# Rotary rows of the input projections in chunks of their own, and operands parked in DRAM as (halves, rows, heads)

## The chip, the cores and the metric

One core of one Trainium2 chip. The time is device microseconds (us) of one execution. TensorE (PE) multiplies matrices; PEld is its weight load; VectorE (DVE), ScalarE (ACT) and GpSimd (POOL) do the elementwise work; SyncE (SP) issues the transfers (DMAs). Below, an instruction is named by its engine and its line in the listing (DVE L782 is VectorE's work on line 782 of the kernel before; the same code stands some 30 lines lower in the kernel after).

## What is computed

A decoder trunk of two layers over 512 tokens of width 1024. Each layer is x += 0.5 SwiGLU(norm x), a mixing stage, and another half-step SwiGLU. The change is in the mixing stage:

```
h = rmsnorm(x, mix_norm[l]) @ w_in[l]                 # 2290 columns
h_a, h_b, h_c = split(h)                              # three groups of heads
o = concat([mla(h_a), nsa(h_b), diff(h_c)]);  x = x + o @ w_out[l]
# nsa:  q (6 heads x 64), kc, ks, kw (2 x 64 each): rotary on the first 16 of 64 dims
# diff: q, k (4 heads x 2 x 32): rotary on the first 8 of 32 dims; then scores,
#       p = p1 - lambda * p2, and p @ v
def apply_rope(x, cos, sin):                          # x1, x2: first and second half of the dims
    return concat([x1 * cos - x2 * sin, x1 * sin + x2 * cos])
```

## The kernel before

Everything is kept transposed: a tile has 128 features on its partitions and the 512 tokens along it. Products in float32 are made of halves: a number is split into a high half (an ACT cast, `split`, L146) and the rest (a subtraction, L148 or, with a scale, L150, on DVE or POOL), and three matrix products are added.

The mixing stage projects 16 chunks of 128 columns of `w_in` (`project`). A projection ends in PSUM and goes through a function `done`. Chunks 3 to 5 hold the queries of the nsa heads, 6 and 7 their keys ks and kw, 8 kc, 9 vc; chunks 12 and 13 hold the queries of the diff heads, 14 and 15 their keys. For chunks 3 to 8 and 12 to 15 `done` is a rotary step (`rope`): a shuffle of partitions from PSUM (DVE L525), PSUM times cos (DVE L526), the shuffled rows times sin (L527) and the sum (L528). The last two run on POOL for chunks 3 to 8 and on DVE for 12 to 15. cos and sin come from DRAM (`tabs`) and are first multiplied by the norm's factor on POOL (`tables`, L535, twice for each of two pairs of tables in a layer). Rows that have no rotary dims go through the same four instructions with cos = 1 and sin = 0. The result is halved and parked in DRAM (`park`, one transfer), and read back in the layout in which the heads need it (`c_load`, `b_queries`, `b_keys`, `compress`).

After the four diff chunks and the values `cv` the program runs through `PLAN`, a table of periods written by hand. A period names the head whose scores are made (front), the head whose probabilities are turned and weighed (back), the order of front steps (f), back steps (b) and other work (.), and what that work is: `p2` or `b8` are projections of chunks, `cl1` is the load of diff head 1, `aq0` a query of the mla heads. Matmuls keep this order; the order on the other engines is made by the compiler's scheduler. The first four periods, c0 to c3, are the diff heads. In each, two softmaxes are combined by DVE L782 (`c_front`), and PE then turns the result (L551) and weighs it (`c_back`).

In layer 1 an ACT table set with exp and ln is preloaded after the last SiLU of the FFN. SyncE issues all transfers in order, and all kinds share its queue: weights, parked tiles, `tabs`.

Of the kernel before, what the change touches and what calls it, by code (L numbers as in the profile page):

```python
# [47 lines left out]

C_ID, C_ONE, C_BLK, C_MSK, C_CM, C_C01, C_FRQ, C_SGN, C_END = 0, 128, 256, 384, 512, 640, 768, 771, 774
# [38 lines left out]
def tile_hybrid_trunk(ctx: ExitStack, tc: tile.TileContext, I, out, dbg=None):  # L88
# [429 lines left out]
    SWAP16 = [(i + 16) % 32 for i in range(32)]  # L518
    SWAP8 = [i + 8 if i < 8 else i - 8 if i < 16 else i for i in range(32)]
    SWAP4 = [i + 4 if i < 4 else i - 4 if i < 8 else i for i in range(32)]  # L520

    def rope(src, cos, sin, swap, r0=0, r1=P, eng=gp):
# [127 lines left out]
    def mix(l, xn, nxt):  # L650
# [45 lines left out]
        def scaled(pj, by):  # L696
            t = tmp()
            ve.tensor_tensor(t, pj, by, op=ALU.mult)
            return t

        def halves(t, scale=None, eng=ve):
            hl = btile()
            n = t.shape[0]
            split(t, hl[:n, 0], hl[:n, 1], scale, eng)
            return hl

        def park(t):
# [30 lines left out]
        def c_init():  # L738
            S["tab"] = tables(2, rs[0])
            dl = small([P, 4, 32], "dl", bufs=1)  # L740
# [13 lines left out]
        def c_done(c, eng=gp):  # L754
            def done(pj):
                if "tab" not in S:
                    c_init()
                S[c] = park(halves(rope(pj, *S["tab"], SWAP4, eng=eng), C_SCALE if c < 14 else None))
            return done

        def c_load(h):
            a, s = h // 2, h % 2
# [166 lines left out]
        def b_rope(c):  # L929
            def done(pj):  # L930
                if "tabb" not in S:
                    S["tabb"] = tables(1, rs[0])
# [3 lines left out]
        def b_token():  # L936
            def done(pj):
                S["b", 9] = park(halves(scaled(pj, rs[0]), eng=gp if "h9" in SPARE else ve))
            return project(9, done)

        def compress(n):
            d, phi, pe_t = (S["b", 8], I["phi_k1"], I["pe_k"]) if n == "k" else (S["b", 9], I["phi_v1"], I["pe_v"])
            pt = small([64, 32], "pe", bufs=1)
# [4 lines left out]
            k = xt.rearrange("p j (g n) -> p j g n", g=2)  # L948
            src = d.rearrange("(g d) j n -> d j g n", g=2)
            pb = ph.unsqueeze(2).broadcast_to([64, 2, 2, 32])  # L950
# [32 lines left out]
        def b_queries(i):  # L983
            q = pair("qk")
            src = S["b", 3 + i].rearrange("(s d) j n -> j d s n", s=2)
            for j in range(2):
                move(q[64 * j:64 * j + 64], src[j])
            S["q", 2 * i], S["q", 2 * i + 1] = q[:, 0], q[:, 1]
# [58 lines left out]
        def b_keys(c, g):  # L1047
            k = S["k", c, g] = btile()
            for d in range(2):
                S["last"] = move(k[64 * d:64 * d + 64], S["b", 6 + c][64 * g:64 * g + 64])  # L1050

# [105 lines left out]
def _consts():  # L1157
# [9 lines left out]
    for t in range(NT):  # L1167
# [4 lines left out]
        c[:, C_C01 + 32 * t:C_C01 + 32 * t + 32] = ok  # L1172
    for g, (inv, per) in enumerate(((INV_A, 32), (INV_B, 64), (INV_C, 32))):
        n = len(inv)
        for p in range(P):
            r = p % per
            if r < 2 * n:
                c[p, C_FRQ + g] = inv[r % n]
                c[p, C_SGN + g] = -1.0 if r < n else 1.0
    return c  # L1180


def _lay(inputs):
# [68 lines left out]
```

## Time and profile before

| | us |
|---|---|
| median of 3 runs | 2050.43 (2048.09 to 2051.41) |
| profiled execution, its own time | 2050.42 |
| its span, first to last instruction | 2048.6 |
| PE busy | 1977.7 |
| DVE busy | 1498.9 |
| ACT busy | 1082.3 |
| POOL busy | 309.6 |

The profiled execution is as good as the median, and 1.8 us of its time lie outside the span. The two mixing stages run from about 361 to 690 us and from about 1373 to 1705 us; the rest is FFN. PE, the engine with the most work, is idle in 70.9 us of the span.

### The profile page before, as it was taken

To read this page: it belongs to the slowest core of one execution; us is meant where nothing else is said; L and a number is where in the kernel's file an instruction comes from. 1 tells how busy PE (TensorE), PEld (TensorE's weight loads), DVE (VectorE), ACT (ScalarE), POOL (GpSimd) and SP (SyncE) were. 2 spreads that over 40 slices of the span, in tenths; PEclk is the share of its full clock that TensorE was granted. 3 is DMA by queue.
4 is the path that set the end of the run, shared out by engine and by line. 5 is a ranking of instruction groups with operands and counts; after the bars stand their busy time and mean duration, and the time that the engine had idled before them with its cause. 6 is when DMAs were issued, how large, how long until landed. Compare 5 with 4: busy or idle time off the path is not lost.

```text
span 2048.6 us, 31102 instructions
## 1 busy us (share of the span) xinstructions
PE 1977.7 (97%) x11864; PEld 1720.7 (84%) x11864; DVE 1498.9 (73%) x2339; ACT 1082.3 (53%) x2023; POOL 309.6 (15%) x217
## 2 busy tenths in 40 slices
PE   8999999978999999999999999999889999999997
PEld 6899988856777899998889999888667778999886
DVE  8888863688897888883378887337888888888623
ACT  4455632476677645562254556225656774555521
POOL 5000011245520100001100000112555110000011
PEclk9999999999999999999999999999989999999999
DMA  6333354623541523335442334446336234233431
GB/s 206 103 108 111 117 180 130 201 91 110 142 155 38 189 93 106 110 118 145 130 134 89 108 107 131 129 138 189 114 100 191 80 124 139 93 104 104 129 116 54
DMA packets 93316, 253.84 MB, mean 124 GB/s; under 512 B 13936, under 2 KB 17776, under 8 KB 93168
## 3 DMA queue, kind: packets, MB, share of 16 engines
q1 hardware_dynamic: 93168, 251.87, 39.6%
q8 instruction: 93, 1.52, 0.3%
q14 instruction: 55, 0.45, 0.1%
HBM read 219.94 MB, written 29.88 MB: 122 GB/s over the span
## 4 chain that ended last, share of the span: by engine, by line
PE 83%; DVE 10%; ACT 3%; POOL 2%; issue 1%; DMA 1%; SPq 0%; DVEq 0%; ACTq 0%; POOLq 0%
PE psm L540 20%; PE psm L175 13%; PE pss L540 11%; PE pst L175 9%; PE pst L540 8%; PE pss L175 8%; PE pso L540 6%; PE pso L175 5%; PE pst L551 1%; DVE pn L782 1%; DVE nmx L573 1%; DVE b L150 1%; DVE pt L148 1%; ACT pn L574 1%; POOL t L270 1%
## 5 line engine op out<-in xcount | busy, mean ns | idle before, releaser
L146 ACT CAST whl<-raw 128x1024 fp32r<-128x1024 f32 (+2 forms) x417 | 383.8, 922 | 512.1 <-issue 107.4
L148 DVE TENSOR_TENSOR whl<-raw,whl 128x512 fp32r<-128x512 f32 (+2 forms) x373 | 409.8, 1100 | 233.3 <-ACT whl L146 232.6
L540 PE MATMUL psm<-b,whl 128*128 128x256 f32 (+1 forms) x2140 | 450.6, 347 | 9.2 <-DVE t L905 8.9
L540 PEld LDWEIGHTS psm<-b,whl 128*128 128x128 f32 x2140 | 329.9, 192 | 51.9 <-DVE t L905 10.7
L270 POOL TENSOR_TENSOR t<-t,t 128x512 f32<-128x512 f32 x48 | 78.8, 1641 | 1104.9 <-ACT t L264 793.8
L175 PE MATMUL psm<-b,whl 128*128 128x512 f32 (+1 forms) x948 | 230.8, 383 | 1.5 <-DVE whl L148 1.0
L175 PEld LDWEIGHTS psm<-b,whl 128*128 128x128 f32 x948 | 174.6, 189 | 36.8 <-DVE whl L148 1.4
L175 PE MATMUL pst<-b,whl 128*128 128x512 f32 x624 | 157.8, 393 | 2.5 <-ACT whl L146 1.3
L574 ACT ACTIVATE pn<-pss,nmx 128x256 f32<-128x256 f32 x208 | 109.9, 529 | 65.7 <-DVE nmx L573 64.5
L175 PEld LDWEIGHTS pst<-b,whl 128*128 128x128 f32 x624 | 117.5, 189 | 29.3 <-ACT whl L146 1.8
L573 DVE TENSOR_REDUCE nmx<-pss 128x1 f32<-128x256 f32 x208 | 97.7, 484 | 40.8 <-PE pss L540 26.5
L175 PE MATMUL pss<-b,whl 128*128 128x512 f32 x504 | 126.4, 389 | 0.0
L540 PE MATMUL psm<-qk,whl 128*128 128x256 f32 x840 | 123.6, 283 | 0.0
L540 PE MATMUL pst<-b,whl 128*128 128x256 f32 (+1 forms) x816 | 121.1, 290 | 0.2 <-DVE b L148 0.2
L540 PE MATMUL pss<-b,whl 128*128 128x256 f32 (+1 forms) x816 | 120.8, 289 | 0.0
L540 PEld LDWEIGHTS psm<-qk,whl 128*128 128x128 f32 x840 | 111.1, 192 | 0.3
L175 PEld LDWEIGHTS pss<-b,whl 128*128 128x128 f32 x504 | 94.6, 188 | 19.6
L540 PEld LDWEIGHTS pst<-b,whl 128*128 128x128 f32 x816 | 108.5, 192 | 2.9 <-DVE b L148 0.5
L540 PEld LDWEIGHTS pss<-b,whl 128*128 128x128 f32 x816 | 108.9, 192 | 2.1
L148 POOL TENSOR_TENSOR whl<-raw,whl 128x1024 fp32r<-128x1024 f32 (+4 forms) x44 | 83.3, 1897 | 172.5 <-ACT whl L146 150.5
L148 DVE TENSOR_TENSOR whl<-pn,whl 128x1024 fp32r<-128x1024 f32 x63 | 77.2, 1225 | 26.3 <-ACT whl L146 26.3
L551 PE MATMUL pst<-cst,pn 128*128 128x128 f32 x440 | 78.0, 292 | 13.0 <-DVE pn L782 7.1
(316 smaller groups left out, 3538.9 us busy)
## 6 DMA issues: line engine op xcount, KB each, us to landing
raw<-in_ffn_gu_dram SPq DMA_DIRECT2D x174, 512.0 KB, 3.7
raw<-in_ffn_d_dram SPq DMA_DIRECT2D x64, 512.0 KB, 3.8
park<-b SPq DMA_DIRECT2D x30, 512.0 KB, 3.7
raw<-in_w_in_dram SPq DMA_DIRECT2D x28, 512.0 KB, 3.7
raw<-in_ffn_d_dram SPq DMA_DIRECT2D x32, 384.0 KB, 3.2
xin<-xs SPq DMA_DIRECT2D x48, 256.0 KB, 3.1
raw<-in_w_out_dram SPq DMA_DIRECT2D x32, 256.0 KB, 2.6
xs<-t SPq DMA_DIRECT2D x24, 256.0 KB, 2.4
```

Source lines behind the costliest of these rows:

```text
L146: high = sc.copy(hi, src) if scale is None else sc.mul(hi, src, scale)
L148: eng.tensor_tensor(lo, src, f32(hi), op=ALU.subtract)
L150: eng.scalar_tensor_tensor(lo, src, scale, f32(hi), op0=ALU.mult, op1=ALU.subtract)
L175: pe.matmul(ps, w(a), x(b), start=first and k == 0 and j == 0, stop=last and k == n - 1 and j == 2)
L270: gp.tensor_tensor(sq, sq, self.acc, op=ALU.add)
L540: return tc.keep_in_program_order(pe.matmul(*args, **kw))
L551: return tc.keep_in_program_order(pe.transpose(dst, src, idn))
L573: ve.reduce_max(nmx, part[i], axis=AX.X, negate=True)
L574: sc.activation(pn[i], part[i], AF.Exp, bias=nmx, accum_out=sm[:, i:i + 1])
L782: ve.scalar_tensor_tensor(p1[j], p1[j], s1[:, j:j + 1], p2[j], op0=ALU.mult, op1=ALU.add)
```

## The change

The columns of `w_in` are put in another order, so that the rotary rows lie together: the diff heads' in chunk 12, the nsa queries' and kc's in chunk 3, the keys' in chunk 6. Only these three chunks get a rotary step (`roped`: PSUM times the norm's factor first, then shuffle, cos, sin and sum out of SBUF, with the plain tables). The other chunks are only multiplied by the norm's factor (`scaled`, one DVE instruction). `tables` and its POOL products go. Scales that differ by row come from a column of constants. Tiles are parked by `put` into tensors shaped (halves, rows, tokens), in which a head's rows lie so that the reads are plain; a chunk is put in two to four pieces. Every diff head now has rows in all four chunks 12 to 15, so that `c_load(0)` stands behind the last of them. `PLAN` swaps b8 with b3 and b3 with b4, and c0 has another order. In `rotary` the last Sin is noted as the activation that the preload has to follow.

```diff
-    ("c0", "", "f.f..fb.f..f.b.bf..bb...", "p2 p0 cl1 cl2"),
-    ("c1", "c0", "f.f..b..ff.f..fbb..bb...", "lat p1 b8 cl3 an"),
+    ("c0", "", "...f.f..f.f..f..f..", "p2 p0 cl1 cl2"),
+    ("c1", "c0", "f.f..b..ff.f..fbb..bb...", "lat p1 b3 cl3 an"),
     ("c2", "c1", "ff....fbf..f.bb..f.bb...", "t9 ak0 av0"),
-    ("c3", "c2", "ff...f.bf.f..bbf..bb...", "b4 aq0 cn0 aq1 b5 b3"),
+    ("c3", "c2", "ff...f.bf.f..bbf..bb...", "b8 aq0 cn0 aq1 b5 b4"),
...
-            sc.activation(h, r, AF.Sin, scale=0.5)
+            last_silu[0] = sc.activation(h, r, AF.Sin, scale=0.5)
...
-    def tables(g, by):
-
-        t = btile(F32)
-        for j in range(2):
-            gp.tensor_tensor(t[:, j], loaded(tabs[g, j]), by, op=ALU.mult)
-        return t[:, 0], t[:, 1]
...
+        def roped(pj, g, swap, n=P, eng=gp):
+
+            t = scaled(pj, rs[0])
+            c, sw = tmp()[:n], tmp()[:n]
+            ve.stream_shuffle(sw, t[:n], swap)
+            ve.tensor_tensor(c, t[:n], loaded(tabs[g, 0])[:n], op=ALU.mult)
+            eng.tensor_tensor(sw, sw, loaded(tabs[g, 1])[:n], op=ALU.mult)
+            eng.tensor_tensor(t[:n], c, sw, op=ALU.add)
+            return t
...
+        def put(part, at, t, r, n):
+
+            return sy.dma_start(part[:, at:at + n].rearrange("j p n -> p j n"), f32(t[r:r + n]))
...
-                S[c] = park(halves(rope(pj, *S["tab"], SWAP4, eng=eng), C_SCALE if c < 14 else None))
+                t = halves(roped(pj, 2, SWAP8, eng=eng) if c == C_TOP else scaled(pj, rs[0]), scales(0))
+                for i in range(2):
+                    put(S["C"][i], 64 * (c - C_TOP), t, 64 * i, 64)
...
-                src = S[12 + 2 * c + a][64 * s:64 * s + 64].rearrange("(m r) j n -> j r m n", m=2)
+                src = S["C"][c].rearrange("j (d h m) n -> j d h (m n)", h=4, m=2)[:, :, h]
+                dst = qk[c].rearrange("p m n -> p (m n)")
                 for j in range(3):
-                    move(qk[c][32 * j:32 * j + 32], src[PASS[j][1 - c]])
+                    move(dst[32 * j:32 * j + 32], src[PASS[j][1 - c]])
...
-                S["b", c] = park(halves(rope(pj, *S["tabb"], SWAP8), B_SCALE if c < 6 else None, gp if "h%d" % c in SPARE else ve))
+                t = roped(pj, 1, SWAP16, P if c == 3 else 64) if c in (3, 6) else scaled(pj, rs[0])
+                scale = {3: scales(1), 8: scales(2), 4: B_SCALE, 5: B_SCALE}.get(c)
+                t = halves(t, scale, gp if "h%d" % c in SPARE else ve)
+                for r, n, p, at in B_PIECES[c]:
...
+                    put(S["part", p], at, t, r, n)
...
-        project2(12, 14)
-        c_load(0)
-        for c in (13, 15):
+        project2(C_TOP, C_TOP + 1)
+        for c in (C_TOP + 2, C_TOP + 3):
             for _ in project(c, c_done(c, ve), ve):
                 pass
+        c_load(0)
```

The order of instructions moves with it at three places. The first is SyncE's queue at the start of the first layer's diff heads: `park` tensors and `part` tensors hold the parked chunks, `qk` tiles are the operands of the heads (two for each head, three reads each). Before:

```order
L710 DMA park_3507<-b_3504 128x1024
L710 DMA park_3518<-b_3515 128x1024
L166 DMA qk_3520<-park_3507 32x2x512 x3
L160 DMA raw_4242<-in_w_a_dram 128x640
L166 DMA qk_3521<-park_3518 32x2x512 x3
L710 DMA park_3567<-b_3564 128x1024
L166 DMA qk_3875<-park_3507 32x2x512
L710 DMA park_3608<-b_3605 128x1024
L166 DMA qk_3875<-park_3507 32x2x512 x2
L166 DMA qk_3876<-park_3518 32x2x512 x3
L166 DMA qk_3883<-park_3567 32x2x512 x3
```
After:

```order
L739 DMA part_3479<-b_3505 64x2x512
L739 DMA part_3480<-b_3505 64x2x512
L739 DMA part_3479<-b_3512 64x2x512
L739 DMA part_3480<-b_3512 64x2x512
L739 DMA part_3479<-b_3549 64x2x512
L739 DMA part_3480<-b_3549 64x2x512
L174 DMA raw_4234<-in_w_a_dram 128x640
L739 DMA part_3479<-b_3586 64x2x512
L739 DMA part_3480<-b_3586 64x2x512
L180 DMA qk_3591<-part_3479 32x1024 x3
L180 DMA qk_3592<-part_3480 32x1024 x3
L180 DMA qk_3864<-part_3479 32x1024 x3
```
The reads of head 0 stood between the first two and the last two chunks; now they stand behind eight pieces of all four.

The second is POOL in the period c1: `whl` are halves of weights, L527 and L528 with 32 rows are the rotary step of the mla key, L183 to L186 an inverse root. Before:

```order
L148 TENSOR_TENSOR whl_4317<-raw_4316,whl_4317 128x1024
L527 TENSOR_TENSOR t_4000<-t_4000,xin_3997 32x512
L820 TENSOR_TENSOR t_3870<-t_3870,t_3989 64x512
L535 TENSOR_TENSOR b_4066<-xin_4067,rstd_3443 128x512
L528 TENSOR_TENSOR t_3999<-t_3999,t_4000 32x512
L535 TENSOR_TENSOR b_4066<-xin_4070,rstd_3443 128x512
L148 TENSOR_TENSOR whl_4440<-raw_4439,whl_4440 128x1024
L527 TENSOR_TENSOR t_4074<-t_4074,b_4066 128x512
L183 TENSOR_TENSOR t_4094<-t_4096 128x512
L528 TENSOR_TENSOR t_4073<-t_4073,t_4074 128x512
L184 TENSOR_TENSOR t_4094<-t_4094,t_4095 128x512
```
After:

```order
L162 TENSOR_TENSOR whl_4309<-raw_4308,whl_4309 128x1024
L540 TENSOR_TENSOR t_3989<-t_3989,xin_3986 32x512
L850 TENSOR_TENSOR t_3859<-t_3859,t_3978 64x512
L541 TENSOR_TENSOR t_3988<-t_3988,t_3989 32x512
L162 TENSOR_TENSOR whl_4428<-raw_4427,whl_4428 128x1024
L713 TENSOR_TENSOR t_4058<-t_4058,xin_4063 128x512
L197 TENSOR_TENSOR t_4086<-t_4088 128x512
L714 TENSOR_TENSOR t_4055<-t_4057,t_4058 128x512
L198 TENSOR_TENSOR t_4086<-t_4086,t_4087 128x512
L200 TENSOR_TENSOR t_4086<-t_4086,t_4088 128x512
```
The two L535 are gone; the rotary step of a projected chunk (L527 and L528 with 128 rows, now L713 and L714) stays, since chunk 3 has taken chunk 8's place here.

The third is DVE where c0 passes into c1: `pss_3893` and `pss_3882` are the first scores of head 1, L782 (L812 after) combines head 0. Before:

```order
L573 TENSOR_REDUCE nmx_3837<-pss_3834 128x1
L776 RECIPROCAL sm_3790<-sm_3790 128x4
L779 TENSOR_SCALAR sm_3790<-sm_3790,nlam_3494 128x4
L782 SCALAR_TENSOR_TENSOR pn_3743<-pn_3743,sm_3744,pn_3789 128x128
L782 SCALAR_TENSOR_TENSOR pn_3743<-pn_3743,sm_3744,pn_3789 128x256
L782 SCALAR_TENSOR_TENSOR pn_3743<-pn_3743,sm_3744,pn_3789 128x384
L698 TENSOR_TENSOR t_3868<-psm_3827,rstd_3443 128x512
L782 SCALAR_TENSOR_TENSOR pn_3743<-pn_3743,sm_3744,pn_3789 128x512
L573 TENSOR_REDUCE nmx_3897<-pss_3893 128x1
L150 SCALAR_TENSOR_TENSOR b_3872<-t_3868,mg_3816,b_3872 128x512
L194 TENSOR_SCALAR t_3906<-pst_3903 128x512
```
After:

```order
L579 TENSOR_REDUCE nmx_3837<-pss_3834 128x1
L806 RECIPROCAL sm_3802<-sm_3802 128x4
L704 TENSOR_TENSOR t_3857<-psm_3797,rstd_3443 128x512
L809 TENSOR_SCALAR sm_3802<-sm_3802,nlam_3489 128x4
L579 TENSOR_REDUCE nmx_3886<-pss_3882 128x1
L164 SCALAR_TENSOR_TENSOR b_3861<-t_3857,mg_3786,b_3861 128x512
L812 SCALAR_TENSOR_TENSOR pn_3750<-pn_3750,sm_3751,pn_3801 128x128
L812 SCALAR_TENSOR_TENSOR pn_3750<-pn_3750,sm_3751,pn_3801 128x256
L812 SCALAR_TENSOR_TENSOR pn_3750<-pn_3750,sm_3751,pn_3801 128x384
L812 SCALAR_TENSOR_TENSOR pn_3750<-pn_3750,sm_3751,pn_3801 128x512
L208 TENSOR_SCALAR t_3895<-pst_3892 128x512
L579 TENSOR_REDUCE nmx_3889<-pss_3882 128x1
```
The combination of head 0 stood ahead of the first reduction of head 1, and now stands behind it and behind a split that waits for ACT (L164).

## Rows read from the trace of the kernel before

**Rows 1.** The page, part 1: busy time, share of the span, instructions.
```profile
PE 1977.7 (97%) x11864; PEld 1720.7 (84%) x11864; DVE 1498.9 (73%) x2339; ACT 1082.3 (53%) x2023; POOL 309.6 (15%) x217
```

**Rows 2.** Windows: length, busy time by engine, granted clock, DMA share, GB/s.
```profile
396.00:566.00 170.00, 145.93 (x767) 112.69 (x768) 140.99 (x254) 115.00 (x265) 86.71 (x57) 0.92 0.44 129
...
664.00:1406.00 742.00, 742.00 (x4569) 670.11 (x4569) 507.28 (x705) 355.10 (x550) 37.45 (x23) 1.00 0.41 126
1406.00:1576.00 170.00, 149.00 (x796) 116.54 (x794) 142.84 (x255) 106.50 (x259) 87.50 (x56) 0.91 0.45 132
```

**Rows 3.** PE's waits, 396 to 566: us, times, longest.
```profile
PE pss L540 <- ACT pn L574: 12.2, 7, 6.0
PE psm L540 <- DVE t L905: 4.8, 2, 3.0
PE pst L551 <- DVE pn L782: 4.6, 3, 2.3
```

**Rows 4.** PE's waits, 1406 to 1576.
```profile
PE pss L540 <- ACT pn L574: 10.7, 4, 5.8
```

**Rows 5.** DVE's timeline: start, us, line, operation, count.
```profile
428.72 6.86 DVE L782 SCALAR_TENSOR_TENSOR pn<-pn,sm,pn 128x128 f32<-128x128 f32 x4 [0.53 <-ACT pn L781]
...
436.72 0.41 DVE L573 TENSOR_REDUCE nmx<-pss 128x1 f32<-128x256 f32 x1
...
457.78 1.93 DVE L782 SCALAR_TENSOR_TENSOR pn<-pn,sm,pn 128x128 f32<-128x128 f32 x4
...
479.16 6.54 DVE L782 SCALAR_TENSOR_TENSOR pn<-pn,sm,pn 128x128 f32<-128x128 f32 x4
485.62 0.74 DVE L150 SCALAR_TENSOR_TENSOR b<-t,dn,b 128x512 fp32r<-128x512 f32 x1
```

**Rows 6.** POOL's timeline at the first and third of the combinations.
```profile
428.29 1.30 POOL L535 TENSOR_TENSOR b<-xin,rstd 128x512 f32<-128x512 f32 x1 [0.24 <-DVE sm L779]
...
477.93 1.86 POOL L527 TENSOR_TENSOR t<-t,b 128x512 f32<-128x512 f32 x1
```

**Rows 7.** DVE by line and form, 396 to 566: count, busy us, mean ns.
```profile
L525 DVE STREAM_SHUFFLE t<-psm 128x512 f32<-128x512 f32 x6 | 4.4, 734 | 0.1
...
L526 DVE TENSOR_TENSOR t<-psm,b 128x512 f32<-128x512 f32 x6 | 4.0, 669 | 0.0
...
L526 DVE TENSOR_TENSOR t<-t,xin 32x512 f32<-32x512 f32 x1 | 2.1, 2120 | 0.0
```

**Rows 8.** POOL by line and form, 396 to 566.
```profile
L528 POOL TENSOR_TENSOR t<-t,t 128x512 f32<-128x512 f32 x6 | 8.6, 1431 | 0.2
...
L527 POOL TENSOR_TENSOR t<-t,b 128x512 f32<-128x512 f32 x6 | 8.3, 1377 | 9.8 <-DVE t L525 8.4 <-issue 1.3
```

**Rows 9.** ACT's timeline: two table loads, and a split of 128x512.
```profile
411.78 1.28 ACT L193 ACT_TABLE_LOAD   x1
413.07 0.69 ACT L193 ACTIVATE t<-pst,epst 128x512 f32<-128x512 f32 x1
413.78 1.28 ACT L574 ACT_TABLE_LOAD   x1
...
479.96 0.70 ACT L146 ACTIVATE b<-t,dn 128x512 fp32r<-128x512 f32 x1
```

**Rows 10.** PE's timeline at the start of the first head.
```profile
383.71 0.43 PE L551 MATMUL pst<-cst,rstd 32*128 32x32 f32 x4
...
396.48 0.41 PE L540 MATMUL pss<-qk,qk 96*128 96x256 f32 x2 [0.64 <-DMA qk<-park]
...
398.01 2.09 PE L540 MATMUL psm<-b,whl 128*128 128x512 f32 x8
```

**Rows 11.** SyncE's timeline there.
```profile
384.01 1.53 SPq L710 DMA_DIRECT2D park<-b  x2
388.83 1.27 SPq L166 DMA_DIRECT2D qk<-park  x3
```

**Rows 12.** Transfers into the `park` tensors: time from issue to landing.
```profile
DMA to landing us min/median/max: 2.4/4.3/8.3
```

More of the change, by code (lines that the diff above doesn't have):

```diff
@@ L518, in tile_hybrid_trunk @@
     SWAP16 = [(i + 16) % 32 for i in range(32)]
-    SWAP8 = [i + 8 if i < 8 else i - 8 if i < 16 else i for i in range(32)]
-    SWAP4 = [i + 4 if i < 4 else i - 4 if i < 8 else i for i in range(32)]
+    SWAP8 = [i + 8 if i % 16 < 8 else i - 8 for i in range(32)]
     def rope(src, cos, sin, swap, r0=0, r1=P, eng=gp):
@@ L711, in park, with parts @@
             return d
+        def parts(n):
+            return dp.tile([2, n, T], F32, name=nm("part"))
+        def put(part, at, t, r, n):
+            return sy.dma_start(part[:, at:at + n].rearrange("j p n -> p j n"), f32(t[r:r + n]))
         def values(w2, key, eng=gp):
@@ L738, in c_init @@
         def c_init():
-            S["tab"] = tables(2, rs[0])
+            S["C"] = [parts(4 * 64) for _ in range(2)]
             dl = small([P, 4, 32], "dl", bufs=1)
@@ L930, in done @@
             def done(pj):
-                if "tabb" not in S:
-                    S["tabb"] = tables(1, rs[0])
-                S["b", c] = park(halves(rope(pj, *S["tabb"], SWAP8), B_SCALE if c < 6 else None, gp if "h%d" % c in SPARE else ve))
+                t = roped(pj, 1, SWAP16, P if c == 3 else 64) if c in (3, 6) else scaled(pj, rs[0])
+                scale = {3: scales(1), 8: scales(2), 4: B_SCALE, 5: B_SCALE}.get(c)
+                t = halves(t, scale, gp if "h%d" % c in SPARE else ve)
+                for r, n, p, at in B_PIECES[c]:
+                    if ("part", p) not in S:
+                        S["part", p] = parts(3 * P if p == "q" else P)
+                    put(S["part", p], at, t, r, n)
             return project(c, done)
[L936 to L939, printed above, removed]
         def compress(n):
-            d, phi, pe_t = (S["b", 8], I["phi_k1"], I["pe_k"]) if n == "k" else (S["b", 9], I["phi_v1"], I["pe_v"])
+            phi, pe_t = I["phi_%s1" % n], I["pe_" + n]
             pt = small([64, 32], "pe", bufs=1)
@@ L948, in compress @@
             k = xt.rearrange("p j (g n) -> p j g n", g=2)
-            src = d.rearrange("(g d) j n -> d j g n", g=2)
+            src = S["part", n + "c"].rearrange("j (d g) n -> d j g n", g=2)
             pb = ph.unsqueeze(2).broadcast_to([64, 2, 2, 32])
@@ L984, in b_queries @@
             q = pair("qk")
-            src = S["b", 3 + i].rearrange("(s d) j n -> j d s n", s=2)
+            src = S["part", "q"][:, P * i:P * i + P].rearrange("j (d s) n -> j d (s n)", s=2)
             for j in range(2):
-                move(q[64 * j:64 * j + 64], src[j])
+                move(q[64 * j:64 * j + 64].rearrange("p s n -> p (s n)"), src[j])
             S["q", 2 * i], S["q", 2 * i + 1] = q[:, 0], q[:, 1]
@@ L1048, in b_keys @@
             k = S["k", c, g] = btile()
-            for d in range(2):
-                S["last"] = move(k[64 * d:64 * d + 64], S["b", 6 + c][64 * g:64 * g + 64])
+            src = S["part", ("ks", "kw")[c]].rearrange("j (d g) n -> g d j n", g=2)[g]
+            for i in range(2):
+                S["last"] = move(k[64 * i:64 * i + 64], src)
         def b_front(h, c):
@@ L1172, in _consts @@
         c[:, C_C01 + 32 * t:C_C01 + 32 * t + 32] = ok
[L1173 to L1179, printed above, removed]
+    rows = {0: [(p, 16) for p in i % 32], 1: [(p, 8) for p in i % 32 // 2], 2: [(C_TURN[p], 4) for p in i % 64 // 8]}
+    for g, inv in enumerate((INV_A, INV_B, INV_C)):
+        for p, (r, n) in enumerate(rows[g]):
+            c[p, C_FRQ + g] = inv[r % n]
+            c[p, C_SGN + g] = -1.0 if r < n else 1.0
+    c[:, C_SCL:C_END] = 1.0
+    c[:64, C_SCL] = C_SCALE
+    c[:96, C_SCL + 1] = B_SCALE
+    c[:32, C_SCL + 2] = B_SCALE
     return c
@@ L1203, in _lay @@
     part = {n: list(range(kv + 128 * j, kv + 128 * j + 128)) for j, n in enumerate(("kc", "vc", "ks", "vs", "kw", "vw"))}
-    rest = list(range(192, 320)) + bq + part["ks"] + part["kw"] + part["kc"] + part["vc"] + part["vs"] + part["vw"] + list(range(C, C + 768))
+    order = {n: list(np.array(part[n]).reshape(2, 64).T.ravel()) for n in ("kc", "ks", "kw", "vc")}
+    order["q"] = list(np.array(bq).reshape(3, 2, 64).transpose(0, 2, 1).ravel())
+    b_cols = [i for k in range(3, 10) for _, m, n, at in B_PIECES[k] for i in order[n][at:at + m]]
+    c_all = np.arange(C, C + 512).reshape(2, 8, 4, 8)
+    c_all[:, :, 0] = c_all[:, :, 0, C_TURN]
+    c_cols = list(c_all.transpose(2, 0, 3, 1).ravel())
+    rest = list(range(192, 320)) + b_cols + part["vs"] + part["vw"] + c_cols + list(range(C + 512, C + 768))
     w = np.concatenate([wi[:, :, cols], wi[:, :, gates], pad, wi[:, :, rest]], 2)
```

14 lines of the change are left out of this document (10 added, 4 removed), and 6 rows, old and new, of the table B_PIECES.

## Prediction

> **What bounds the kernel now.** The first view is the page's busy times: PE works 97% of the span [rows 1]. The change leaves the matrix products as they are, so that PE's 1977.7 us stay, and only two things can move the time: the stretches in which PE waits, and the clock it is granted. The windows say where those are. Between the mixing stages PE is busy for all of 742 us at a granted clock of 1.00; in the stretches with the diff heads it is idle for 170.00 - 145.93 = 24.1 us in layer 0 and 170.00 - 149.00 = 21.0 us in layer 1, and the granted clock is 0.92 and 0.91 there [rows 2]. The reader should see two prices: the idle time itself, and work done at the lower level (1.2 instead of 2.4 GHz in part of the stretch), which is up to 145.93 x 0.08 + 149.00 x 0.09 = 25.1 us. The other stages have nothing to give.
>
> Next come PE's waits in these stretches. In layer 0, 12.2 us end with ACT's exponential (L574, 6.0 us at once), 4.6 with DVE's combination of two softmaxes (L782), 4.8 with DVE L905 [rows 3]; in layer 1 the longest of the first kind is 5.8 us [rows 4]. Then DVE's timeline at the two largest gaps. Both begin with the four L782: they take 1.93 us at 457.78, but 6.86 us at 428.72 and 6.54 us at 479.16 [rows 5]. The reduction (L573) for which the exponential waits stands behind the first of these, at 436.72, and PE waits through it. POOL's timeline shows what is different there: at 428.29 and 477.93 POOL is in the middle of rotary products (L535, L527) [rows 6]. So the wait named after ACT is made by DVE, and DVE is slow where POOL is busy.
>
> **POOL's work.** Per layer the diff tables (two L535, 1.30 us each) and the nsa tables (two more) go, and four of the six pairs L527 and L528 in these stretches, since only chunks 3 and 6 keep a rotary step: 4 x (1.377 + 1.431) = 11.2 us [rows 8], and the two L535 in c1, 2.6 us; 13.8 of POOL's 86.71 us [rows 2, 6].
>
> That DVE and POOL hinder each other here is read from the rows: a DVE product with one operand in PSUM takes 0.669 us, and the one of two SBUF operands took 2.120 us though it has a quarter of the rows [rows 7]. The Trainium skill ("SBUF — State Buffer", Who interferes with whom) gives the rule: a DVE instruction with two SBUF inputs contends with a GpSimd instruction that reads SBUF, and one with at most one such input does not. By that rule the stretched L782 fit, and it also speaks against this change: the new rotary step takes cos out of SBUF (L712), where PSUM times cos was safe before.
>
> **Gap 1, in c1, both layers.** The two L535 go; a pair of L527/L528 stays in this place (chunk 3 now). The four L782 then lose at least the two L535, 2.6 us, if they go on alternating with POOL's other work, and at most all that is over 1.93 us, 4.9 us [rows 5, 6]. I take the middle, 3.8. Against that the rotary step has one DVE instruction more, the norm's product, 0.67 us [rows 7], and L712 may be held up: nothing to 2.120 - 0.669 = 1.5 us; I take 0.6, since POOL is busy for half of the stretch (86.71 of 170) and has less to do now. Net -2.5 us per layer (bounds -4.2 and -0.4).
>
> **Gap 2, where c2 passes into c3.** A plain chunk comes through here now. L527 (1.86 us) and L528 (1.43) leave POOL, so the 6.54 us become 3.3 at most and 1.93 at least, and DVE loses a shuffle of 0.73 us and has one product as before [rows 5 to 8]. PE waits 4.6 us for L782 [rows 3], nearly all of it in this gap: I take -3.2, and -0.5 more from the waits for L905, which sit on the same DVE queue. -3.7 per layer (bounds -1.5 and -6).
>
> **The start of c1.** DVE's order puts the combination of head 0 behind a reduction (0.41 us) and behind a split whose cast is ACT's: 0.70 and 0.74 us [rows 5, 9]. +1.85 us per layer if PE has no other work there; PE's own order is the cover, and without it this is the price. In layer 0 two ACT table loads stand just ahead, 1.28 us each [rows 9], and go, because the set with exp and ln is now preloaded behind the last Sin in layer 0 as it was behind SiLU in layer 1: -2.57. Net -0.7 in layer 0, +1.85 in layer 1 (bounds: nothing, to +3.2 where the split is stretched as L782 was). Most other table loads stand where ACT waits anyway: nothing. The next ACTIVATE begins 1.29 us after the load starts [rows 9]. The Trainium skill ("ScalarE: Activation LUTs", What ACT_TABLE_LOAD costs) adds a drain and counts about 2.66 us for a switch; by that the term would be -5.3, and the row does not bear it out.
>
> **Operands by way of DRAM.** Eight pieces replace four tiles, and the reads of head 0 stand behind all eight. Before, the second of the tiles for head 0 was issued at about 384.8 (half of the pair at 384.01), the first read went out at 388.83, and the first score ran at 396.48, 11.7 us after [rows 10, 11]. Now the last chunk leaves PE at 383.71; its product, cast and subtraction, 0.67 + 0.70 + 0.74, and one other instruction on DVE give 387, and the second piece some 0.77 us later. Counted on: 387.8 + 11.7 = 399.5, less 0.8 because the six reads now go in one piece and no weight stands among them: 398.7. The score was wanted at 396.48 - 0.64 = 395.84; the new order of c0 has three dots of projection first, 12 matmuls of 2.09 / 8 = 0.26 us, so that it is wanted at 399.0. I take 0, and -0.6 in layer 0 for the wait of 0.64 us that goes. The cover is thin: each of the two hops, usually 4.3 us, may take 8.3 [rows 12], and then up to 8 us a layer appear. Behind the reads wait those of head 1 and the weights of the next chunks, but those are wanted later. In front of c0 DVE has eight instructions fewer per layer (sixteen before; now one for each of four chunks and four more for one): 8 x 0.67 = 5.4 us of DVE's time, but PE's products of the values cover it, from 384 to 395.84: nothing; uncovered it would be a gain of as much.
>
> **The sum.** Layer 0: -2.5 - 3.7 - 0.7 - 0.6 = -7.5; layer 1: -2.5 - 3.7 + 1.85 = -4.4 (rounded). Together -11.9 us of PE's idle time. Clock: 25.1 us of slower work against 45.1 us of idle time is 0.56 us for each idle us; I take half, since the mean clock counts the idle stretches too and not every gap has to do with it: -3.3. In all -15.2. The profiled execution took 2050.42 us, as good as the median of the three runs: 2050.4 - 15.2 = 2035.2, so 2035.
>
> **The rivals.** (a) *The relief is taken back.* DVE's 141 us of 170 in the stretch are nearly its bound [rows 2]; if the stretched instructions only move to L164, L712 and the weight halves of the periods beside, PE's wait moves with them. For it: POOL keeps 73 of 87 us, and L712 has two SBUF operands. Against it: the largest gaps have named places whose POOL work leaves. The time is then about 2050, within 4 us.
> (b) *Head 0's operands come late: slower.* If a put takes the 8.3 us of the slowest landing and the reads as much, +8 us per layer: -11.9 + 16 = +4.1, with the clock's 0.28 in proportion +5.3, so 2055.7. It decides from some 6 us per layer on. For it: everything of c0 waits for the last of eight pieces in a queue that runs in order. Against it: the median hop is 4.3, and bytes are the same.
> (c) *The gaps go altogether.* If both stretched groups fall to 1.93 and PE's waits for L574, L782 and L905 in layer 0 (21.6 us) and about as much in layer 1 fall by two thirds, some 28 us go, and with them half of the clock's loss: 28 to 35 us, 2015 to 2022. For it: the waits are few and all hang on DVE. Against it: the reductions and exponentials of a head stay in series.
> (d) *The preload does not follow the Sin*: the table loads then stay, and layer 0 loses its -2.6 alone: 2038, inside the likeliest case.
>
> **How the numbers follow.** The forecast with (d) has 0.60, with a range of its own of 2024 to 2043, from the bounds of the gaps and of c1's start; (a) 0.12; (b) 0.13; (c) 0.15. A measurement of this kernel tells 0.2%, 4.1 us, from no change: 2046.3 and 2054.5 are the borders. Faster: 0.60 + 0.15 = 0.75; same 0.12; slower 0.13. The range reaches from the middle of (c), 2017, to the near end of (b), 2052; what is left out is half of (c) and most of (b), under 2 in 10.
>
> **What would show it.** Right: the two L812 groups that were 6.86 and 6.54 us are under 4.5; PE's longest wait for the exponential in each stretch falls from 6 to about 3; PE's idle time in the two stretches falls from 45 to about 33 us; no table load in layer 0's heads; PE waits less than a microsecond for the first score. Wrong: a wait of PE on a transfer of `part` at c0 (rival b); L712 at 2 us with PE waiting behind it, or the same idle time under other lines (a); a granted clock that does not rise although the idle time falls would take the last 3.3 us away.

## Result and profile after

The kernel after takes 2032.72 us (median of 4 runs, 2027.59 to 2033.53), the one before 2050.92 (4 runs): a ratio of 0.9908 with a 95% interval of 0.9888 to 0.9928, 18 us or 0.9% faster. 2035 was forecast.

The page of after, its first part (engine, busy time, share, instructions), to be read against [rows 1]:

```profile
PE 1973.1 (97%) x11864; PEld 1713.7 (84%) x11864; DVE 1474.7 (73%) x2305; ACT 1066.4 (53%) x2010; POOL 281.5 (14%) x193
```

PE's products are the same 11864. The span fell by 18.4 us (2048.6 to 2030.2): PE's idle time by 13.8 (70.9 to 57.1), and its busy time by 4.6, for the same products at a higher granted clock (next rows). DVE has 34 instructions less, POOL 24 and ACT 13; the last are the table loads.

The windows of the two stretches of the same length, beside [rows 2] (layer 1 begins 13 us earlier now):

```profile
396.00:566.00 170.00, 152.80 (x838) 118.41 (x837) 145.50 (x277) 113.11 (x280) 80.48 (x53) 0.95 0.55 158
1393.00:1563.00 170.00, 154.40 (x855) 120.98 (x854) 140.77 (x264) 110.66 (x269) 79.30 (x49) 0.94 0.53 150
```

Idle time is 17.2 and 15.6 us instead of 24.1 and 21.0, the granted clock 0.95 and 0.94 instead of 0.92 and 0.91. PE's waits in layer 0's stretch (us in total, times, longest), beside [rows 3]:

```profile
PE pss L546 <- ACT pn L580: 8.1, 6, 3.2
PE pst L557 <- DVE pt L162: 2.9, 3, 2.2
PE pso L546 <- DVE pt L162: 2.8, 2, 2.2
PE psm L546 <- DVE t L935: 1.8, 1, 1.8
PE pst L557 <- DVE pn L812: 0.9, 3, 0.3
```

The waits for the exponential fell from 12.2 to 8.1 us, those for the combination (L782, now L812) from 4.6 to 0.9. What grew, from 1.5 to 5.7 us, is PE's wait for the split of turned probabilities (L148, now L162): 2.15 us at the split of head 0, where it was 1.09, and 2.24 us behind gap 2.

DVE's timeline at the two places, beside [rows 5]:

```profile
428.49 2.27 DVE L812 SCALAR_TENSOR_TENSOR pn<-pn,sm,pn 128x128 f32<-128x128 f32 x4 [0.53 <-ACT pn L811]
...
433.23 1.67 DVE L712 TENSOR_TENSOR t<-t,xin 128x512 f32<-128x512 f32 x1
434.82 1.28 DVE L873 TENSOR_SCALAR gate<-gate 128x128 f32<-128x128 f32 x1
...
437.00 0.69 DVE L579 TENSOR_REDUCE nmx<-pss 128x1 f32<-128x128 f32 x2
...
478.61 1.93 DVE L812 SCALAR_TENSOR_TENSOR pn<-pn,sm,pn 128x128 f32<-128x128 f32 x4
```

Both groups of four L812 are near the undisturbed 1.93 us. But the first sits in front of something new: L712, the cos product with two operands in SBUF, takes 1.67 us, and the gate's product behind it (L873) 1.28. The reduction L579 that PE's wait ends with, by way of the exponential, comes only at 437.00. POOL there:

```profile
426.20 1.61 POOL L541 TENSOR_TENSOR t<-t,t 32x512 f32<-32x512 f32 x1
431.82 2.53 POOL L162 TENSOR_TENSOR whl<-raw,whl 128x1024 fp32r<-128x1024 f32 x1 [4.01 <-issue]
```

POOL has finished L541 just before the L812 begin, and rests for 4 us; its subtraction for the weights then runs from 431.82, under L712. PE's timeline at the start of head 0, at its split, at the end of gap 1, at the next wait for the exponential and behind gap 2; the last line is the end of gap 1 in layer 1:

```profile
395.51 2.91 PE L546 MATMUL psm<-b,whl 128*128 128x512 f32 x12
398.26 0.39 PE L546 MATMUL pss<-qk,qk 96*128 96x256 f32 x2
...
427.33 0.78 PE L546 MATMUL pso<-pt,b 128*64 128x384 f32 x5 [2.15 <-DVE pt L162]
...
437.78 0.79 PE L546 MATMUL pss<-qk,qk 96*128 96x512 f32 x1 [3.24 <-ACT pn L580]
...
458.76 0.50 PE L546 MATMUL pss<-qk,qk 96*128 96x512 f32 x1 [2.75 <-ACT pn L580]
...
484.73 0.52 PE L557 MATMUL pst<-cst,pn 128*128 128x128 f32 x2 [2.24 <-DVE pt L162]
...
1441.62 0.51 PE L546 MATMUL pss<-qk,qk 96*128 96x512 f32 x1 [2.59 <-ACT pn L580]
```

Three dots of projection cover the way by DRAM: the first score starts at 398.26 without a wait (forecast: wanted at 399.0, ready at 398.7). Gap 1 is 3.24 us instead of 6.0 (in layer 1 2.59 instead of 5.8). The next wait of its kind has grown from 1.90 us:

```profile
459.07 0.50 PE L540 MATMUL pss<-qk,qk 96*128 96x512 f32 x1 [1.90 <-ACT pn L574]
```

That line is from the kernel before; after the change the wait is 2.75 us, and in layer 1 3.19 instead of 1.90.

### The profile page after: what moved, and what is told of

It is laid out like the page before. It is cut to its first block, busy times and chain, and to the rows that moved or that the text cites. A ratio compares the mean times of both kernels' runs of the same rounds, so it can differ in the third digit from the quotient of the medians.

```text
span 2030.2 us, 31058 instructions
## 1 busy us (share of the span) xinstructions
PE 1973.1 (97%) x11864; PEld 1713.7 (84%) x11864; DVE 1474.7 (73%) x2305; ACT 1066.4 (53%) x2010; POOL 281.5 (14%) x193
## 3 DMA queue, kind: packets, MB, share of 16 engines
q8 instruction: 93, 1.52, 0.3%
## 5 line engine op out<-in xcount | busy, mean ns | idle before, releaser
L162 DVE TENSOR_TENSOR whl<-raw,whl 128x512 fp32r<-128x512 f32 (+2 forms) x373 | 408.9, 1098 | 237.0 <-ACT whl L160 236.2
L579 DVE TENSOR_REDUCE nmx<-pss 128x1 f32<-128x256 f32 x208 | 97.2, 484 | 35.1 <-PE pss L546 24.1
L162 POOL TENSOR_TENSOR whl<-raw,whl 128x1024 fp32r<-128x1024 f32 (+4 forms) x44 | 81.5, 1854 | 208.3 <-ACT whl L160 196.7
L162 DVE TENSOR_TENSOR whl<-pn,whl 128x1024 fp32r<-128x1024 f32 x63 | 77.1, 1224 | 26.6 <-ACT whl L160 26.6
```

The costliest lines, as they stand in the source:

```text
L162: eng.tensor_tensor(lo, src, f32(hi), op=ALU.subtract)
L579: ve.reduce_max(nmx, part[i], axis=AX.X, negate=True)
```

## Experiments

All times are medians beside runs of the kernel before on the same chip (2050 to 2052 us). "Over after" means against 2032.7. Products called dead are added work whose result, in a tile `dead` of its own, nobody reads; no run leaves work out. Inserted lines shift line numbers by two to nine. Each timeline and list of waits is that of one run of the kernel, not of the median one.

**b_sin: the table loads alone.**

```diff
 (before)
-            sc.activation(h, r, AF.Sin, scale=0.5)
+            last_silu[0] = sc.activation(h, r, AF.Sin, scale=0.5)
```

> The kernel before with one line of the change: the last Sin is noted, so that the preload of the exp and ln table set follows it in layer 0. The order on the other engines stays. My theory (what is gained comes mostly from POOL's products leaving the places where DVE is stretched, and from fewer DVE instructions): the table loads of layer 0's heads go, the time falls by 2 to 4 us, to about 2048, and the two stretched groups of L782 stay at 6 to 7 us. Rival (the table loads were the gain of layer 0): the time falls by 8 us or more, layer 0's stretch loses 8 of its 24 us of idle time.

2044.83 us, ratio 0.9971 (0.9960 to 0.9981): 5.4 us faster, between the two theories. PE's waits in layer 0's stretch, beside [rows 3]:

```profile
PE pss L540 <- ACT pn L574: 8.6, 5, 5.9
PE pst L551 <- DVE pt L148: 3.6, 1, 3.6
PE psm L540 <- DVE t L905: 3.4, 2, 1.8
```

Gap 1 is all but unchanged (5.9 us at once), so the loads within it cost next to nothing. Gone are waits of 0.74 and 0.65 us at the head of c1 and one of 1.91 us at 518.86, in a later period, and a wait for L905 fell from 2.98 to 1.52. DVE's combination in c1 starts 2.9 us earlier, counted from the start of the values `cv`, close to the 2.57 us of two loads that were forecast; the rest is later. Not all of it is kept: behind gap 2 a wait of 3.62 us for the split L148 is new, in place of 2.27 us for L782.

**a_nosin: the same line taken out of the kernel after.**

```diff
 (after)
-            last_silu[0] = sc.activation(h, r, AF.Sin, scale=0.5)
+            sc.activation(h, r, AF.Sin, scale=0.5)
```

> The kernel after without its line that notes the last Sin, so that the table loads of layer 0's heads come back. From the kernel before with that line alone (5.4 us faster, 3 of them ahead of c1 and the rest in the later periods) I expect the same price here if it adds up with the others: 4 to 7 us slower than the kernel after, about 2038, all in layer 0. Rival (the loads are covered once DVE and POOL have less to do): within 2 us of the kernel after.

2038.70 us, 0.9936 (0.9921 to 0.9951): 6 us over after, though its runs spread (2033.8 to 2043.6) and its interval just overlaps that of after (0.9888 to 0.9928). The two prices agree as far as that goes, and there is no sign that the rest of the change covers the loads.

**b_plan: the order written by hand, alone.**

```diff
 (before)
-    ("c0", "", "f.f..fb.f..f.b.bf..bb...", "p2 p0 cl1 cl2"),
-    ("c1", "c0", "f.f..b..ff.f..fbb..bb...", "lat p1 b8 cl3 an"),
+    ("c0", "", "...f.f..f.f..f..f..", "p2 p0 cl1 cl2"),
+    ("c1", "c0", "f.f..b..ff.f..fbb..bb...", "lat p1 b3 cl3 an"),
...
-    ("c3", "c2", "ff...f.bf.f..bbf..bb...", "b4 aq0 cn0 aq1 b5 b3"),
+    ("c3", "c2", "ff...f.bf.f..bbf..bb...", "b8 aq0 cn0 aq1 b5 b4"),
```

> The kernel before with the new PLAN alone (order of c0, chunk 3 in c1, chunks 8 and 4 in c3), all chunks with the rotary step and the old tables. My theory: all of these chunks are alike here, so that the time moves by no more than 3 us either way; the first score's wait of 0.64 us goes. Rival (the order written by hand is what was gained): 9 us or more of the 18 are there, and PE's longest wait for the exponential falls from 6 to about 3 us.

2054.73 us, 1.0021 (1.0011 to 1.0032): 4.5 us slower. The order alone gives nothing in time. Yet DVE's first group shrank in layer 0, with both L535 still on POOL (this profile is of the slowest of twelve runs, 2060.3 us):

```profile
430.96 3.51 DVE L782 SCALAR_TENSOR_TENSOR pn<-pn,sm,pn 128x128 f32<-128x128 f32 x4 [0.53 <-ACT pn L781]
```

3.5 us instead of 6.9, and PE's longest wait for the exponential is 3.4 us, as the rival had it:

```profile
PE pss L540 <- ACT pn L574: 11.2, 7, 3.4
PE pst L551 <- DVE pn L782: 5.0, 5, 2.4
```

In layer 1 it did not: the group takes 5.66 us there, and the wait is 4.8 us. In layer 0 the sum of that kind of wait fell by 1 us only (12.2 to 11.2), gap 2 stayed, and the granted clock of the stretch was 0.90. So the length of one gap says little: it depends on where DVE meets POOL, and the time comes back at other places.

**a_gap1 and a_gaps: POOL's work put back.** Two dead products stand in c1 where the two L535 stood in POOL's order; a_gaps adds two for each of the chunks 4, 5, 7 and 8, which lost their rotary step. DVE has the same instructions as in after, but not quite their order: in c1 the split of 32 rows (L162 at 431.39 in after) stands behind the cos product in both runs, and the reduction that gap 1 ends with stands ahead of the gate's reciprocal; in a_gaps some instructions ahead of the combinations of gap 2 are in another order too.

```diff
 (after; both kernels, in rope)
         eng.tensor_tensor(sw, sw, sin[r0:r1], op=ALU.mult)
+        for j in range(2):
+            gp.tensor_tensor(dead[r0:r1], sw, sin[r0:r1], op=ALU.mult)
 (a_gaps only, in b_rope)
+                if c in (4, 5, 7, 8):
+                    for j in range(2):
+                        gp.tensor_tensor(dead, t, rs[0], op=ALU.mult)
```

> The kernel after with two products more on POOL in c1 (and wherever the mla key takes its rotary step), whose result nobody reads: they stand in POOL's order where the two table products (L535) stood in the kernel before. The order on DVE stays. My theory: the four L812 that took 2.3 us in c1 are stretched again, to 4 to 7 us, PE's wait for the exponential there grows from 3.2 to 5 or 6 us, and the time rises by 4 to 8 us for both layers with the clock. Rival (POOL's work is harmless, DVE was late for its own number of instructions, or the order was what helped): nothing, within 2 us.

2034.86 us, 0.9921 (0.9907 to 0.9935): 2.1 us over after, with intervals that overlap. POOL's timeline in c1, the dead products being L544:

```profile
427.00 1.60 POOL L544 TENSOR_TENSOR dead<-t,xin 32x512 f32<-32x512 f32 x1
428.57 1.27 POOL L545 TENSOR_TENSOR t<-t,t 32x512 f32<-32x512 f32 x1
429.80 1.27 POOL L544 TENSOR_TENSOR dead<-t,xin 32x512 f32<-32x512 f32 x1
433.49 2.40 POOL L164 TENSOR_TENSOR whl<-raw,whl 128x1024 fp32r<-128x1024 f32 x1 [2.41 <-issue]
```

and DVE's:

```profile
428.53 1.34 DVE L813 TENSOR_SCALAR sm<-sm,nlam 128x4 f32<-128x4 f32 x1
430.40 2.41 DVE L816 SCALAR_TENSOR_TENSOR pn<-pn,sm,pn 128x128 f32<-128x128 f32 x4 [0.53 <-ACT pn L815]
```

The L816 (L812 of after) stay at 2.41 us: POOL is idle from 431.07 to 433.49. The dead products met DVE earlier, at L813 (1.34 us for a 128x4 tile that takes 0.23 in after), and DVE came to the combinations 1.1 us later, counted from the start of `cv`. PE's gap 1 was 2.2 us, no longer than in after. My theory of gap 1, that the missing L535 are what keeps these combinations short, is not borne out. Nor is this a full replay: in the kernel before, the L535 and the weight subtraction behind them ran under the combinations, and here the dead products end 0.7 us after the combinations begin. The shorter gap may also be the reduction's new place.

> As the run with two more products in c1, and also two products on POOL, read by nobody, for each of the chunks 4, 5, 7 and 8 that lost their rotary step: POOL has about as much to do as before. My theory: besides gap 1, the group of L812 where c2 passes into c3 is stretched from 1.93 to 4 us or more; the time rises by 9 to 15 us over the kernel after, most of what was gained. Rival (DVE's smaller number of instructions and the order are the gain): no more than 4 us over the kernel after.

2043.89 us, 0.9970 (0.9960 to 0.9980): 11.2 us over after, 9.0 over a_gap1. Gap 2 is back. DVE:

```profile
481.83 1.69 DVE L166 SCALAR_TENSOR_TENSOR b<-t,b 128x512 fp32r<-128x512 f32 x1
483.45 5.22 DVE L816 SCALAR_TENSOR_TENSOR pn<-pn,sm,pn 128x128 f32<-128x128 f32 x4
```

POOL at the same time (L968 is a dead product):

```profile
481.25 1.73 POOL L164 TENSOR_TENSOR qk<-t,qk 96x512 fp32r<-96x512 f32 x1
482.94 1.70 POOL L968 TENSOR_TENSOR dead<-t,rstd 128x512 f32<-128x512 f32 x1
484.61 2.33 POOL L164 TENSOR_TENSOR whl<-raw,whl 128x1024 fp32r<-128x1024 f32 x1
```

and PE behind it:

```profile
487.24 1.31 PE L561 MATMUL pst<-cst,pn 128*128 128x128 f32 x3 [4.72 <-DVE pn L816]
```

The four combinations take 5.22 us instead of 1.93, and PE waits 4.72 us for them, with the number of DVE's instructions unchanged. The clock has its part: from 484 to 500 us the granted clock is 0.57, and in a_gap1 0.89; the matching 16 us of layer 1 have the same pair. This is the cleaner half of the test: POOL's products in that place, with the order that the scheduler then made on DVE, cost gap 2.

**a_gaps_sh: the shuffles too.** As a_gaps, with a shuffle on DVE ahead of each pair, as before the change.

```diff
 (a_gaps)
                 if c in (4, 5, 7, 8):
-                    for j in range(2):
-                        gp.tensor_tensor(dead, t, rs[0], op=ALU.mult)
+                    sw = tmp()
+                    ve.stream_shuffle(sw, pj, SWAP16)
+                    gp.tensor_tensor(dead, sw, rs[0], op=ALU.mult)
+                    gp.tensor_tensor(dead, t, sw, op=ALU.add)
```

> The kernel after with POOL's two products in c1, and for each of the plain chunks 4, 5, 7 and 8 a shuffle on DVE and two products on POOL behind it, all of whose results nobody reads: nearly the elementwise work of the kernel before, without its wait for the sum. The run without the shuffles took 2043.9 us. If DVE's smaller number of instructions is the rest of the gain (the kernel before with the noted Sin took 2044.8, and has no stretched L712), this one is 5 us or more above 2043.9. Rival (the shuffles are hidden, the rest of the gain is that the splits no longer wait for POOL's sum): within 3 us of 2043.9.

2044.00 us, 0.9966 (0.9953 to 0.9978): the rival. The shuffles of the plain chunks, 4 x 0.73 us of DVE a layer, are hidden here.

**a_c0old: the old order of c0.**

```diff
 (after)
-    ("c0", "", "...f.f..f.f..f..f..", "p2 p0 cl1 cl2"),
+    ("c0", "", "f.f..fb.f..f.b.bf..bb...", "p2 p0 cl1 cl2"),
```

> The kernel after with the old order of c0, whose first step is a score. PE then wants head 0's operands at about 395.5 us, and they land at about 398: a wait of 2 to 4 us per layer for a transfer of the parts, about 2037 to 2042 in all. Two theories of gap 1: if the missing L535 keep the four L812 of c1 short (my prediction), they stay at about 2.3 us; if it is the order of c0, which brings these L812 ahead of POOL's products (the old kernel with the new PLAN had 3.5 instead of 6.9 us with the L535 still there), they are stretched to 3.5 us or more and PE's wait for the exponential in c1 is over 4 us.

2032.68 us, 0.9915 (0.9901 to 0.9930): no difference, a miss. The wait is there, and is given back:

```profile
398.09 0.41 PE L546 MATMUL pss<-qk,qk 96*128 96x256 f32 x2 [2.28 <-DMA qk<-part]
...
427.11 0.79 PE L546 MATMUL pso<-pt,b 128*64 128x384 f32 x5 [1.10 <-DVE pt L162]
```

PE waits 2.28 us for the parts at 398.09, and then 1.10 instead of 2.15 us at the split of head 0, and less at its scores, as if DVE and ACT, not PE, bound c1's start. The parts are there at 398.1, where 398.7 was forecast. On gap 1, the combinations took 2.42 us and the gap was 3.36, in both layers: without L535 and with the old order of c0 it is short as well. The new PLAN alone (b_plan) nearly halves it in layer 0 only. L712 took 2.14 us in this run, longer than the 1.67 of after, at the same time in all.

**a_psum: the rotary step out of PSUM.** The norm's product is written in place in PSUM for the full chunks (12 and 3; chunk 6 stays), so that the cos product has one operand in SBUF.

```diff
 (after, in roped)
-            t = scaled(pj, rs[0])
+            t = tmp() if n == P else scaled(pj, rs[0])
+            u = pj if n == P else t
+            if n == P:
+                ve.tensor_tensor(pj, pj, rs[0], op=ALU.mult)
...
-            ve.stream_shuffle(sw, t[:n], swap)
-            ve.tensor_tensor(c, t[:n], loaded(tabs[g, 0])[:n], op=ALU.mult)
+            ve.stream_shuffle(sw, u[:n], swap)
+            ve.tensor_tensor(c, u[:n], loaded(tabs[g, 0])[:n], op=ALU.mult)
```

> The kernel after, where the full rotary chunks (12 and 3) are multiplied by the norm's factor in place in PSUM, and shuffle and cos product read PSUM: DVE's cos product (L712) then has one operand in SBUF, as before the change. If contention of two SBUF operands with POOL stretches L712 in c1 (1.67 us), it falls to about 0.7, PE's wait for the exponential in c1 from 3.2 to about 2.2, and the time by 1 to 3 us. Rival (its length has another cause, or the gate's two instructions behind it set the wait): L712 or the wait stays, and the time is within 1 us, or longer because the PSUM bank is held longer.

2016.42 us, 0.9829 (0.9817 to 0.9842): 16.3 us under after, far more than the 1 to 3 expected. DVE's timeline in c1:

```profile
434.63 0.69 DVE L715 TENSOR_TENSOR t<-psm,xin 128x512 f32<-128x512 f32 x1
435.24 0.30 DVE L876 TENSOR_SCALAR gate<-gate 128x128 f32<-128x128 f32 x1
435.46 0.74 DVE L579 TENSOR_REDUCE nmx<-pss 128x1 f32<-128x128 f32 x2
```

L715 is the cos product: 0.69 us where POOL's weight subtraction runs beside it (432.96 to 435.46), and the gate's product 0.30. The reduction for the next score comes at 435.46 instead of 437.00. PE's waits for the exponential in the stretch:

```profile
PE pss L546 <- ACT pn L580: 3.6, 6, 1.0
```

Gap 1 is gone (8.1 to 3.6 us in all), the granted clock is 0.97. The next wait of the kind fell as well, from 2.75 to 0.94 us (in layer 1 from 3.19 to 0.93). Not all of this is the length of L712, since the scheduler moved more: that reduction ahead of the gate's reciprocal, on ACT three activations of an inverse root (L194 to L196) behind the exponentials, and the combinations of head 1, which begin at 447.98 us instead of 454.41, in three pieces.

**a_bold and a_both: the old places of the nsa chunks**, that is, a plain chunk in c1 and the rotary one at the end of c3; a_both has a_psum's edit too.

```diff
 (after; a_both: a_psum)
-    ("c1", "c0", "f.f..b..ff.f..fbb..bb...", "lat p1 b3 cl3 an"),
+    ("c1", "c0", "f.f..b..ff.f..fbb..bb...", "lat p1 b8 cl3 an"),
...
-    ("c3", "c2", "ff...f.bf.f..bbf..bb...", "b8 aq0 cn0 aq1 b5 b4"),
+    ("c3", "c2", "ff...f.bf.f..bbf..bb...", "b4 aq0 cn0 aq1 b5 b3"),
```

> The kernel after with the old places of the nsa chunks in PLAN: 8 in c1, and 4 and 3 in c3. The rotary step with its POOL products and its L712 moves from c1 to the end of c3. My theory: gap 1 loses the 1.7 us of L712 (PE's wait for the exponential in c1 falls from 3.2 to about 2), and the end of c3 gets that work; in all within 4 us of the kernel after. Rival (the places are what keeps gap 2 closed): the L812 where c2 passes into c3 are stretched to 4 us or more, and the time is 5 us or more above the kernel after.

2018.77 us, 0.9844 (0.9831 to 0.9856): 14 us under after, a miss of both theories (no stretched group at gap 2, and a gain beyond 4 us). PE's waits in layer 0's stretch:

```profile
PE pss L546 <- ACT pn L580: 2.9, 5, 1.3
PE psm L546 <- ACT t L209: 2.2, 1, 2.2
```

The waits for the exponential fell from 8.1 to 2.9 us; the end of c3 pays with 2.2 us (L209), and with 1.8 us more just behind it.

> The rotary step out of PSUM (2016.4 us) together with the old places of the nsa chunks (2018.8 us). If both gain because they take the same instruction, L712 with its two SBUF operands, out of POOL's way in c1, they don't add: 2013 to 2021. If they gain by different things, about 2004 (14 us below the first).

2020.95 us, 0.9851 (0.9838 to 0.9864): they don't add. That is what the forecast has for two edits that take the same thing away, the price of the rotary step in c1. It does not prove it, for in this run too the end of c3 pays with some 3.7 us of waits in layer 0 and 5.1 in layer 1.

**a_ps_sb and a_ps_ps: is it the length or the location?** On top of a_psum one dead product in chunk 3, from SBUF or from PSUM, at the same place of DVE's order.

```diff
 (a_psum, in roped, behind the cos product)
+            if n == P and g == 1:
+                ve.tensor_tensor(dead, sw, rs[0], op=ALU.mult)      # a_ps_sb
+                ve.tensor_tensor(dead, pj, sw, op=ALU.mult)         # a_ps_ps instead
```

> The kernel with the rotary step out of PSUM, and in chunk 3 one product more on DVE that nobody reads, of two SBUF operands (the shuffled rows and the norm's factor); it stands on DVE two reductions behind the cos product. To be compared with its twin, whose product stands at the same place and has one operand in PSUM. If the location of the operands is what costs, this product takes 1.3 us or more where POOL is busy, the twin's 0.7, and this kernel is 1 to 6 us slower than the twin. Rival (any further instruction on DVE there costs the same): both within 2 us of each other, and both slower than 2016 by 2 us or more.

> The twin: the same product at the same place on DVE, of one operand in PSUM and the shuffled rows. If the location of the operands is what costs: about 0.7 us long, the time within 2 us of 2016.4. Rival (the number of instructions on DVE): 2 us or more above 2016.4, as its twin.

2026.89 (0.9866 to 0.9896) and 2024.58 us (0.9856 to 0.9883): 10.5 and 8.2 us over a_psum, within 2.3 us of each other with overlapping intervals. The two dead products:

```profile
436.51 0.68 DVE L719 TENSOR_TENSOR dead<-t,rstd 128x512 f32<-128x512 f32 x1
```

```profile
435.38 0.67 DVE L719 TENSOR_TENSOR dead<-psm,t 128x512 f32<-128x512 f32 x1
```

Both took 0.68 us, so neither met POOL, and the pair says nothing on the location. It could not: POOL's next product takes the shuffled rows in place, and so waits in both runs until the dead product has read them, in a_ps_sb so:

```profile
437.27 1.28 POOL L720 TENSOR_TENSOR t<-t,xin 128x512 f32<-128x512 f32 x1 [1.43 <-DVE dead L719]
```

What the pair says is that one product a layer of 0.68 us, together with the 1.43 us for which it holds up POOL, costs 8 us in two layers. The waits for the exponential in layer 0 with the twin:

```profile
PE pss L548 <- ACT pn L582: 6.3, 7, 2.7
```

6.3 us against a_psum's 3.6 (the twin's runs lie between 2021.8 and 2027.2, and this is the profile of the fastest). The longest, 2.7 us, is the one that a_psum had at 0.94; ahead of it the last of head 1's combinations takes 1.67 us beside a split on POOL, which had begun before it, and 0.75 in a_psum, where it begins first.

## Why the prediction came out right

The direction and size are right: 2032.7 for 2035, idle time -13.8 for -11.9, PE's busy time (the clock's part) -4.6 for -3.3. By its own steps:

- *Gap 2* (-3.7 a layer): the size is right. The wait for L782 fell by 3.7 us in layer 0 and by 2.1 in layer 1. The wait for L905 that was to lose 0.5 us lost 3.0 and 2.3; b_sin shows that the table loads alone account for half of the 3.0. Against it stands a new wait of 2.2 us for L162 in layer 0, and 0.4 us more of it in layer 1. That POOL's products make gap 2 is shown by a_gaps, but for the order on DVE that moved with them: a price of 9 us for both layers, where the sum had 7.4 and its share of the clock.
- *Gap 1* (-2.5 a layer): the size is right, 2.8 us in layer 0 and 3.2 in layer 1 (5.8 to 2.6), in part by luck: in layer 0 the four combinations lost 4.6 us where 3.8 was taken, and L712 with the gate's product cost 1.3 where 0.6 was taken. The cause is not shown: "the four L782 then lose at least the two L535" was not borne out by the dead products in their place, which left the group at 2.41 us, and in layer 0 the new PLAN alone shortened it with L535 in place. What the traces show is that these instructions are short where DVE comes to them while POOL rests. Nor is all of it kept: the next wait of the kind grew by 0.9 and 1.3 us, which is rival (a) in small.
- *L712 in that term* (+0.6): mis-sized. It is 1.0 us longer itself, the gate's product behind it 0.3, and both stand ahead of the reduction. Taking it out of the way, with what the scheduler then moved, is worth 16 us for both layers. The rule of the Trainium skill ("SBUF — State Buffer", Who interferes with whom) pointed at this instruction, and the trace agrees: 1.67 us with two operands in SBUF, 0.69 with one in PSUM, POOL reading beside both. The prediction's wording, that at most one operand in SBUF is safe, is wider than that section, which excepts the 2-port modes; and in a_gap1 a 128x4 product (L813), whose only other operand is a column of scalars, was stretched beside POOL. Whether it ran in such a mode no run shows.
- *Start of c1 and the table loads* (-0.7 in layer 0, +1.85 in layer 1): the two loads were about right, 2.9 us for 2.57, but "most other table loads stand where ACT waits anyway: nothing" failed. The line is worth 5.4 to 6 us. Of the 1.85 us for the new order, 1.1 can be seen as a wait of PE, at the split of head 0 (1.09 to 2.15 us, in layer 1 to 2.16).
- *The way by DRAM* (0, and -0.6): right. Layer 0's first score had no wait, layer 1's one of 0.5 us. Rival (b), late operands, was priced too high: in a_c0old a wait of 2.3 us in layer 0 and 2.5 in layer 1 cost nothing.
- *The shuffles*, to which gap 2's term gives no price of their own: right by a_gaps_sh.

So the mechanism of gap 2 held, and the total was met partly by luck, with terms that erred in both directions: the loads gave more; POOL's products of the plain chunks gave about what was forecast; the rotary step in c1 costs far more than its own instructions. Three single prices, 5.4 (loads), 9.0 (POOL's products of the plain chunks) and 2.1 (those in c1, unresolved), add up to 16.5 of the 18.2 us. That they add is not shown: b_plan and a_c0old show that a wait which goes in one place may come back in another. What stays open is what shortened gap 1, and how much of a_psum's 16 us is the length of L712 and how much the order that follows from it; a run in which only the order differs was not made.

The best version is a_psum, 2016.42 us, 1.7% under the kernel before and 0.8% under the one after.

## What to carry to other kernels

When a gap ends with one engine, look at what stretched the instruction ahead of that wait: here the same four DVE instructions took 1.93 us where POOL rested and 6.9 where it worked beside them. Moving an operand from PSUM to SBUF is not free where POOL reads SBUF, even when the instruction count falls. And a wait found on PE need not be worth its length, since it can come back at another place: put the wait back alone before booking its price. A dead instruction is no pure price either: see what waits for it, and whether the scheduler moved others.

## What was not expected of the hardware

In the chain of scores, exponentials and combinations a short DVE instruction has leverage: one of 0.68 us a layer, with the 1.43 us for which POOL waited for it, cost 8 us in two layers (2016.4 to 2024.6), while 2.3 us of PE waiting in layer 0 and 2.5 in layer 1 at the start of c0 cost nothing. Part of what a stretch gains is the clock: with less idle time the granted clock of layer 0's stretch rose from 0.92 (before) over 0.95 (after) to 0.97 (a_psum), and PE's whole busy time for the same 11864 products fell from 1977.7 to 1973.1 to 1966.3 us. And a 128x4 product on DVE, 0.23 us alone, took 1.34 us beside POOL's products in a_gap1, so that a small size is no guard against this.
